# Four low parts of folded weights by TensorE and ScalarE, and layer 1's first statistics three products later

## The chip, the cores and the metric

The kernel runs on one core of one Trainium2 chip. The metric is the device time of one execution in microseconds (us). A core has five engines with instruction queues of their own: TensorE (PE; its weight loads are shown as PEld), VectorE (DVE), ScalarE (ACT), GpSimd (POOL) and SyncE (SP, which only issues transfers here). Each works through its queue in order and waits on semaphores for the others.

## The reference

A decoder trunk of two layers on x (1024 positions of width 1024), conditioned on a vector c. In short:

```python
c_act = silu(c)
for l in range(2):
    shift, scale, gate = split(c_act @ ada_w[l] + ada_b[l], 3)
    if l == 0:                                   # gated multi-scale causal pooling
        h = rmsnorm(x, norm_g[0]) * (1 + scale) + shift
        u, z = split(h @ w_in, 2)                # each 1024 x 2048
        p = trailing_mean(u, windows=(2, 4, 8, 16)) - u
        y = (einsum("sgc,gcd->sgd", p, w_group) * a_scale * silu(z)) @ w_out
    else:                                        # sliding-window attention, window 128, 16 heads
        k, v = from hk = modulated rmsnorm(x) @ w_kv   # shared K and V
        h = rmsnorm(x, norm_g[1]) * (1 + scale) + shift
        q, z = split(h @ b_w_in, 2)
        y = (attention(q, k, v, bias, sinks) * silu(z)) @ b_w_out
    x = x + gate * y
out = rmsnorm(x, final_g)
```

Pooling is linear along the positions, so for the first channel group the product of `w_in` and `w_group` can be formed ahead (`w_in @ w_group`, the "folded weights" below) and applied to h at once.

## The kernel before, in words

x is held transposed, as 8 tiles `xk[k]` of 128 channels by 1024 positions, and most work is done for two halves q of 512 positions. Every fp32 product is made of three passes of a faster format: a matrix is split in a high part (the value rounded to that format) and a low part (the rest), and high by high, high by low and low by high are summed in PSUM. "A product" below is one such pass, a 128x512 matmul.

The start. While x arrives, TensorE forms the folded weights for group 0: eight matrices `jb[m]` of 128x512 in PSUM banks (`join_mm`, line 629), each out of four chunks `ci` of `wu` and `wg`. Each is then split: `joined_h(m)` (line 634) copies it to SBUF as the high part by ScalarE, and `joined_l(m)` (line 639) subtracts that from the bank as the low part by VectorE. Meanwhile ScalarE squares x (715), VectorE sums the squares (720, 724), and for each half `rstd_stats` brings the sums over channels to PSUM (478, tiny matmuls against a column), VectorE adds the epsilon (`v`, 481), GpSimd raises it to the power -1/2 (`rs`, 483), and `rstd_spread` (490) spreads it over the partitions, from where ScalarE copies it (813 for the first half, 830 for the second). The shifts and scales of the adaptive norm are dot products of a loaded row block with silu(c) by VectorE (`ada_dot`, line 557; its bias comes from `pk`, a packed tile of small vectors; silu(c) is line 765, on the broadcast `cact`). Then for each k in 4, 0, ... the input of layer 0 is built for both halves: scaling (677, 680, VectorE), high part (682, ScalarE), low part (686, VectorE), and used at once in 12 products per k and half (`first_mm`, line 700) in the order (0,0), (0,1), (4,0), (4,1), (1,0) and so on.

Then follow layer 0's other products, its output projection in two parts (`ps_d` and others by line 985 and 530), and, before layer 1, the last chunks of the output projection for the second half of positions (`last_chunk`, 12 products each). Into their row on TensorE are put layer 1's first statistics (`rstd_stats` on `sqh[0]`) and their spread, whose result `rb` scales x for K, V and the queries.

What sets the order: up to the K and V products everything is noted first (`nc.noting`) and written out by a planner, `in_list`. TensorE's instructions keep the order of the source text. Those of ScalarE and VectorE are taken by a due time, `want`, counted back from the products that need them with estimated lengths; SP's transfers too. Instructions called through `at(t, f, ...)` near layer 1 are sorted by t ahead of that. Buffers are taken from rings by name, so an order also decides who waits for a buffer. From K and V on, a second list with its own planner follows; the change does not touch it.

Of the kernel before, what the change touches and what calls it, by code (L numbers as in the profile page):

```python
# [15 lines left out]
F32 = mybir.dt.float32  # L16
# [5 lines left out]
P = 128  # L22
# [80 lines left out]
LAG = {PE: 0.25, ACT: 0.15, DVE: 0.12, POOL: 0.12, SP: 0.0}  # L103


class Tile:


    def __init__(self, home, steps, on):
        self.home, self.steps, self.on = home, steps, on  # L110
# [100 lines left out]
class Step:  # L211
    def __init__(self, at, engine, length, kb, f, due):
        self.at, self.engine, self.length, self.kb, self.f = at, engine, length, kb, f
        self.due, self.lag = due, LAG[engine]
        self.needs, self.next, self.held, self.done, self.ready = set(), [], False, None, 0.0


# [67 lines left out]
def in_list(notes, begin):  # L285

    t = begin
    for n in notes:
        for m in n.needs:
            m.next.append(n)  # L290
        if n.engine == PE:
            n.want = t
            t += n.length
    left = {n: len(n.next) for n in notes}
    last_first = [n for n in notes if not left[n]]
    for n in last_first:
        for m in n.needs:
            left[m] -= 1
            if not left[m]:
                last_first.append(m)  # L300
    assert len(last_first) == len(notes)
    for n in last_first:
        if n.engine != PE:
            n.want = min([t + n.due] + [m.want for m in n.next]) \
                - n.length - n.lag - (n.kb / 250 + 2.0 if n.kb else 0.0)
    queue = [n for n in notes if n.engine == PE][::-1]
    by_want = {e: sorted((n for n in notes if n.engine == e), key=lambda n: (n.want, n.at))
               for e in (ACT, DVE)}
    left = {n: len(n.needs) for n in notes}
    free = dict.fromkeys(LAG, 0.0)  # L310
    free[PE], landed = begin, 0.0
    waiting = {e: [n for n in notes if n.engine == e and not left[n]] for e in LAG}

    def sooner(n, now):

        late = max(0.0, free[PE] - queue[-1].want) if queue else 0.0
        some = [m for m in by_want[n.engine][:40] if m.done is None and m.want < n.want][:10]
        for m in some:
            ready = now
            for o in m.needs:  # L320
                if o.done is not None:
                    ready = max(ready, o.done + o.lag)
                elif o.engine == PE:
                    ready = max(ready, max(o.want + late, free[PE]) + o.length + o.lag)
                else:
                    break
            else:
                end = now + n.length
                if now < ready < end - 0.05 and m.want + late < end < n.want + late - m.length:
                    return ready  # L330
        return None

    for _ in notes:
        while True:
            best = None
            for e, some in waiting.items():
                if e == PE:
                    some = queue[-1:] if queue and not left[queue[-1]] else []
                if some:
                    at = max(free[e], min(n.ready for n in some), landed - 2.5 if e == SP else 0.0)  # L340
                    n = min((n for n in some if n.ready <= at), key=lambda n: (n.want, n.at))
                    if best is None or at < best[0]:
                        best = at, n
            at, n = best
            then = None if n.held or n.engine not in by_want else sooner(n, at)
            if then is None:
                break
            n.held, free[n.engine] = True, then
        n.begin = at
        (queue.pop() if n.engine == PE else waiting[n.engine].remove(n))  # L350
        if n.engine in by_want:
            by_want[n.engine].remove(n)
        free[n.engine] = n.done = at + n.length
        if n.kb:
            landed = max(landed, n.done)
            landed += n.kb / (390 if 7.0 < landed < 45.0 else 300)
            n.done = landed + 2.0
        for m in n.next:
            left[m] -= 1
            m.ready = max(m.ready, n.done + (n.lag if m.engine != n.engine else 0.0))  # L360
            if not left[m] and m.engine != PE:
                waiting[m.engine].append(m)
    return sorted(notes, key=lambda n: (n.begin, n.at))
# [3 lines left out]
def trunk(ctx, tc, xT, x_again, c, pack, ada_first, ada_rest, wu0_in, wg0_in, wa, wg, wao, wkv,  # L367
          wb, wbo, bias_in, fg_row, outT, out_last):
    nc = Work(tc.nc)
    mm = nc.tensor.matmul  # L370
# [14 lines left out]
    def bank(tag):  # L385
        return pp.tile([P, H], F32, tag=tag, name="ps_" + tag, bufs=BANKS[tag])
# [23 lines left out]
    ident = cp.tile([P, P], F32, name="ident")  # L410
# [75 lines left out]
    def rstd_spread(rs, n):  # L486

        bc = bank("tp")
        for j in range(n):
            mm(bc[:, j * P:(j + 1) * P], rs[:, j:j + 1].broadcast_to([P, P]), ident,  # L490
               start=True, stop=True)
        return bc

    sqh = [None, None]
# [39 lines left out]
    with ExitStack() as sa:  # L534
# [10 lines left out]
        def slot(name):  # L545
            if not slots_at:
                slots_at.append(ap.tile([P, SLOT_FILL], F32, name="fill2"))
            return ap.tile([P, 2, H], F32R, tag="wo", name=name, bufs=4)
# [87 lines left out]
        def joined_l(*ms):  # L636
            for m in ms:
                w = w0[m // 2][:, m % 2]
                nc.vector.tensor_sub(out=w[:, 1, :], in0=jb[m], in1=w[:, 0, :].bitcast(F32))

        def dots(k, i, gain=True):
            ada_dot(ads[k][i], cact, 8 * i + k, C_ADAB + 8 * i + k)
# [48 lines left out]
        def first_mm(k, q, passes=(0, 1, 2)):  # L691
            if k == 0 and 0 in passes:
                for i in range(4):
                    psu[i, q] = bank(("d", ("tp", "o", "S", "S")[i])[q])
            order = [(s, i) for s in passes for i in range(4)]
            if (k, q) == (KT - 1, 1):
                order.sort(key=lambda e: e[1])
            for s, i in order:
                w, hl = ((0, 0), (1, 0), (0, 1))[s]
                mm(psu[i, q], w0[k // 2][:, k % 2, w, i * P:(i + 1) * P],  # L700
                   moving(block(k, q)[hl]),
                   start=k == 0 and s == 0, stop=k == KT - 1 and s == 2)
# [29 lines left out]
        nc.scalar.dma_start(raw0[:, half(0)], wu0_in[0, :, half(0)])  # L732
        fetch_c(0)
        nc.sync.dma_start(pk, pack)
        nc.sync.dma_start(cact, c.broadcast_to([P, T]))
        fetch_c(1)
        fetch_ada(0)
# [8 lines left out]
        def warm(n):  # L746

            some = ones.broadcast_to([P, P])
            for _ in range(n):
                mm(warm_bank[:, :P], some, some, start=True, stop=True)  # L750
# [3 lines left out]
                join_mm(m, jb[m], ci, s)  # L754

        warm(10)
        jb = [bank(t) for t in ("d", "d", "d", "d", "S", "S")]
        split_wg(0)
        split_wu(0, half(0), nc.vector.tensor_copy)
# [65 lines left out]
        first_l(0, 0)  # L825
        dots(4, 0, False)
        joined_h(7)
        joined_l(7)
        bc = rstd_spread(rs, 4)
        nc.scalar.copy(out=rbs[1], in_=bc)  # L830
        first_mm(0, 0)
        first_h(0, 1)
        dots(4, 1, False)
# [269 lines left out]
        w = split_w(*first_raw)  # L1103
# [6 lines left out]
        w = load_w(wa[17])  # L1110
# [109 lines left out]
        def g_acts(k, hl, q):  # L1220
            return moving(g_parts[8 + k, q][:, hl, :])
# [19 lines left out]
        for i, (kind, g, j) in enumerate(steps):  # L1241
            w, nxt = nxt, pair_w(*steps[i + 1]) if i + 1 < len(steps) else None
# [61 lines left out]

        late = list(range(LATE, KT))[::-1]

        def last_chunk(i):

            n, c = late[i // 2], i % 2
            if c == 0:  # L1310
                got[n] = bank(("S", "d")[i // 2 % 2])
            passes([(1, got[n])], ws[n], c * 512,
                   lambda k, hl, q: g_acts(4 * c + k, hl, q), 4, c == 0, c == 1)


        xrs = {}
# [34 lines left out]
        rb = slot("rb")[:, 0, :].bitcast(F32)  # L1351
        hk0 = Modulated(0, rb, 8, 48)
        h10 = Modulated(0, rb, 16, 24)
        got = {}
        plan = []

        def at(t, f, *args, due=12.0):
            plan.append((t, len(plan), f, args, due))

        def put(k, f, *args):  # L1360
            got[k] = f(*args)
# [22 lines left out]
        NT = 12 * 0.2157  # L1384
# [6 lines left out]
            at(t + 0.05, take_h, key, due=-0.2)  # L1391
            at(t + 1.3, take_l, key, due=0.2)
        for i in range(nl):
            at(NT * i, last_chunk, i)
            if i % 2 == 1:
                t, n = NT * (i + 1), late[i // 2]
                at(t + AFTER[0], lambda n: residual(n, 1, got[n], 16), n, due=3.0)
                at(t + AFTER[1], square_s, n, 1, due=3.0)
                at(t + AFTER[2], square_a, n, 1, due=3.0)
        assert rest_at[0] == len(rest_cols)  # L1400
        at(NT - 0.01, lambda: put("st", rstd_stats, sqh[0], 4))
        at(2 * NT - 0.01, lambda: nc.scalar.copy(out=rb, in_=rstd_spread(got["st"], 4)))
        for i in range(16):
            m = (hk0, h10)[i // 8]
            t = 2 * NT + STEP[0] + STEP[1] * i
# [989 lines left out]
```

## Time and profile before

| | us |
|---|---|
| median of 3 runs | 901.51 (901.36 to 901.70) |
| the profiled execution: time | 901.06 |
| the profiled execution: span, first to last instruction | 899.4 |
| TensorE busy | 889.5 (99%) |
| VectorE busy | 755.8 (84%) |
| ScalarE busy | 506.5 (56%) |
| GpSimd busy | 160.5 (18%) |
| mean granted TensorE clock | 0.998 |

Busy time of TensorE counts a product from its start to the end of its pipeline, so rows that follow one another overlap; a short wait hides in that. Lines are given as L and the number in the kernel before; the changed kernel has other numbers for the same statements (by 1 at the start, by 5 to 9 later).

### The profile page before, as it was taken

To read this page: it belongs to the slowest core of one execution; us is meant where nothing else is said; L and a number is where in the kernel's file an instruction comes from. 1 tells how busy PE (TensorE), PEld (TensorE's weight loads), DVE (VectorE), ACT (ScalarE), POOL (GpSimd) and SP (SyncE) were. 2 spreads that over 40 slices of the span, in tenths; PEclk is the share of its full clock that TensorE was granted. 3 is DMA by queue.
4 is the path that set the end of the run, shared out by engine and by line. 5 is a ranking of instruction groups with operands and counts; after the bars stand their busy time and mean duration, and the time that the engine had idled before them with its cause. 6 is when DMAs were issued, how large, how long until landed. Compare 5 with 4: busy or idle time off the path is not lost.

```text
span 899.4 us, 13251 instructions
## 1 busy us (share of the span) xinstructions
PE 889.5 (99%) x4486; PEld 787.3 (88%) x4486; DVE 755.8 (84%) x1411; ACT 506.5 (56%) x1074; POOL 160.5 (18%) x263
## 2 busy tenths in 40 slices
PE   9999999999999999999999999999999999999996
PEld 8788888888888888888888888888998888998996
DVE  6999989877988899698986789489999966779785
ACT  7546435333444335483353459488897656677643
POOL 0100000000000000000000000234434545456651
PEclk9999999999999999999999999999999999999999
DMA  9742451573248624998697966945777565465032
GB/s 360 275 140 94 166 209 48 190 244 127 94 171 310 255 84 141 320 345 305 223 325 272 338 239 231 321 152 204 237 258 274 186 204 166 159 194 184 16 141 105
DMA packets 65843, 186.80 MB, mean 208 GB/s; under 512 B 8168, under 2 KB 16496, under 8 KB 65776
## 3 DMA queue, kind: packets, MB, share of 16 engines
q1 hardware_dynamic: 56208, 151.88, 48.0%
q0 software_dynamic: 8992, 32.51, 10.9%
q10 hardware_dynamic: 576, 1.57, 0.5%
q8 instruction: 35, 0.57, 0.2%
q14 instruction: 32, 0.26, 0.1%
HBM read 138.48 MB, written 41.95 MB: 201 GB/s over the span
## 4 chain that ended last, share of the span: by engine, by line
PE 92%; DMA 4%; DVE 2%; issue 0%; ACT 0%; SPq 0%; DVEq 0%; ACTq 0%
PE ps_d L985 18%; PE ps_d L1581 9%; PE ps_d L1583 9%; PE ps_d L1582 9%; PE ps_S L985 9%; PE ps_d L530 9%; PE ps_tp L985 4%; PE ps_o L985 4%; PE ps_S L530 3%; PE ps_tp L530 2%; PE ps_o L530 2%; PE ps_d L700 2%; PE ps_o L1823 2%; PE ps_S L1736 2%; PE ps_tp L1773 2%; PE ps_S L1735 2%
## 5 line engine op out<-in xcount | busy, mean ns | idle before, releaser
L955 ACT CAST ws<-tw 128x512 fp32r<-128x512 f32 x68 | 41.5, 619 | 65.0 <-DVE tw L960 33.3
L985 PE MATMUL ps_d<-hs,ws 128*128 128x512 f32 x312 | 71.6, 379 | 0.0
L557 DVE CUSTOM_DVE_ANT_0 tmp<-tmp,cact,pk 128x1024 f32<-128x1024 f32 x48 | 60.6, 1278 | 9.0 <-DMA tmp<-ada_rest 9.0
L1581 PE MATMUL ps_d<-hm,wh 128*128 128x512 f32 x176 | 67.8, 385 | 0.0
L1582 PE MATMUL ps_d<-hm,wh 128*128 128x512 f32 x176 | 66.7, 379 | 0.0
L1583 PE MATMUL ps_d<-hm,wl 128*128 128x512 f32 x176 | 66.7, 379 | 0.0
L985 PEld LDWEIGHTS ps_d<-hs,ws 128*128 128x128 f32 x312 | 59.0, 189 | 8.4
L1750 ACT ACTIVATE P<-P,nm 128x129 f32<-128x129 f32 x128 | 50.1, 394 | 26.9 <-DVE nm L1746 26.6
L985 PE MATMUL ps_d<-ha,ws 128*128 128x512 f32 x252 | 57.8, 379 | 0.0
L872 POOL MEMSET tmp<- 128x16 f32 x12 | 1.3, 111 | 312.3 <-DMA kept_g<-tmp 137.1
L1791 POOL TENSOR_SCALAR_AFFINE_SELECT pp<-ph 128x512 fp32r<-128x512 f32 x54 | 46.1, 870 | 58.6 <-DVE ph L1779 38.4
L985 PEld LDWEIGHTS ps_d<-ha,ws 128*128 128x128 f32 x252 | 47.6, 189 | 6.8
L956 DVE TENSOR_TENSOR ws<-tw,ws 128x512 fp32r<-128x512 f32 x68 | 45.7, 683 | 7.3 <-ACT ws L955 7.2
L1791 POOL TENSOR_SCALAR_AFFINE_SELECT ph<-ph 128x512 fp32r<-128x512 f32 x56 | 45.5, 827 | 0.0
L956 DVE TENSOR_TENSOR ws<-raw,ws 128x512 fp32r<-128x512 f32 x51 | 34.7, 683 | 10.1 <-ACT ws L955 10.0
L1761 ACT ACTIVATE P<-P,den 128x128 f32<-128x128 f32 x128 | 40.6, 389 | 2.0 <-DVE den L1757 2.0
L483 POOL TENSOR_TENSOR rs<-v,mhalf 128x4 f32<-128x4 f32 x3 | 5.0, 1656 | 203.4 <-DVE v L481 203.4
L530 PE MATMUL ps_d<-gh,wh 128*128 128x512 f32 x128 | 40.9, 380 | 0.0
L955 ACT CAST ws<-raw 128x512 fp32r<-128x512 f32 x51 | 31.4, 620 | 12.1 <-issue 5.5
L1746 DVE CUSTOM_DVE_ANT_0 P<-ps_S,bias,nsink 128x128 f32<-128x128 f32 x128 | 37.7, 345 | 0.4
L1583 PEld LDWEIGHTS ps_d<-hm,wl 128*128 128x128 f32 x176 | 33.3, 189 | 4.7
L1581 PE MATMUL ps_d<-hm,raw 128*128 128x512 f32 x96 | 37.2, 387 | 0.0
(372 smaller groups left out, 2688.7 us busy)
## 6 DMA issues: line engine op xcount, KB each, us to landing
tmp<-ada_rest SPq DMA_DIRECT2D x48, 512.0 KB, 4.6
raw<-wa SPq DMA_DIRECT2D x28, 512.0 KB, 3.5
raw<-wao SPq DMA_DIRECT2D x21, 512.0 KB, 5.2
raw<-kw POOLq DMA_DIRECT2D x20, 512.0 KB, 4.3
wh<-kw POOLq DMA_DIRECT2D x19, 512.0 KB, 3.6
wl<-kw POOLq DMA_DIRECT2D x19, 512.0 KB, 4.6
ad<-ada_first SPq DMA_DIRECT2D x16, 512.0 KB, 4.4
kept_g<-tmp SPq DMA_DIRECT2D x16, 512.0 KB, 4.1
```

The lines of the kernel that those rows point to most:

```text
L530: mm(p, lhs, acts(k, hl, q), start=start and k == ks[0] and s == 0, stop=stop and k == ks[-1] and s == 2)
L557: nc.vector.tensor_tensor_reduce(out=raw, in0=raw, in1=ca, scale=1.0, scalar=pk[:, bcol:bcol + 1], op0=ALU.mult, op1=ALU.add, accum_out=ad ...
L955: nc.scalar.copy(out=ws[i][:, 0, :], in_=src)
L956: nc.vector.tensor_sub(out=ws[i][:, 1, :], in0=src, in1=ws[i][:, 0, :].bitcast(F32))
L985: mm(ps, lhs, acts(k, hl), start=start and k == 0 and s == 0, stop=k == 3 and s == 2, skip_group_check=True)
L1581: mm(p, lh, a[0](), start=k == 0, stop=False)
L1582: mm(p, lh, a[1](), start=False, stop=False)
L1583: mm(p, ll, a[0](), start=False, stop=k == n - 1)
L1746: note(DVE, 0.28, lambda: nc.vector.tensor_tensor_reduce(out=pt()[:, i, :P], in0=s()[:, e, :P], in1=bias[:, hd, :], scale=-1.0, scalar=nsi ...
L1750: note(ACT, 0.41, lambda: nc.scalar.activation(pt()[:, i, :P + 1], pt()[:, i, :P + 1], AF.Exp, bias=nm()[:, i:i + 1], scale=-1.0, accum_ou ...
L1761: note(ACT, 0.3, lambda: nc.scalar.activation(pt()[:, i, :P], pt()[:, i, :P], AF.Copy, scale=den()[:, i:i + 1]), [(den, i)], [(pt, i)])
L1791: note(POOL, 0.85, lambda: nc.gpsimd.affine_select(out=v8(to(), h), in_=v8(cur(), h).bitcast(F32), pattern=[[0, 2], [0, 4], [-sign, 2], [- ...
```

## The change

Four of the eight low parts, m = 2, 3, 6 and 7, are made by another way: TensorE multiplies the high part with a negated identity matrix (`less`) and adds this onto the bank, which leaves the low part there, and ScalarE copies it to SBUF. The last low part (m = 7) comes behind the second half's spread in the source. The transfer of `pk` gets a due time (`by`), which the planner keeps for it, and is issued ahead of the second half of x. Near layer 1, `last_chunk` is noted in four pieces of three products each instead of one of twelve, and the statistics and their spread are put one such piece, three products, later.

```diff
@@ Step, in_list
-        self.due, self.lag = due, LAG[engine]
+        self.due, self.lag, self.by = due, LAG[engine], float("inf")
...
+            n.want = min(n.want, n.by)
@@ trunk
         def joined_l(*ms):
             for m in ms:
                 w = w0[m // 2][:, m % 2]
-                nc.vector.tensor_sub(out=w[:, 1, :], in0=jb[m], in1=w[:, 0, :].bitcast(F32))
+                if m in (2, 3, 6, 7):
+                    mm(jb[m], less, w[:, 0, :], start=False, stop=True, skip_group_check=True)
+                    nc.scalar.copy(out=w[:, 1, :], in_=jb[m])
+                else:
+                    nc.vector.tensor_sub(out=w[:, 1, :], in0=jb[m], in1=w[:, 0, :].bitcast(F32))
...
         nc.sync.dma_start(pk, pack)
+        nc.notes[-1].by = 14.0
...
         warm(10)
+        less = slot("less")[:, 0, :P]
+        nc.scalar.mul(less, ident, -1.0)
...
         joined_h(7)
-        joined_l(7)
         bc = rstd_spread(rs, 4)
         nc.scalar.copy(out=rbs[1], in_=bc)
+        joined_l(7)
         first_mm(0, 0)
...
-        def last_chunk(i):
+        def last_chunk(i, ks=range(4)):
...
-            at(NT * i, last_chunk, i)
+            for k in range(4):
+                at(NT * (i + k / 4), last_chunk, i, range(k, k + 1))
...
-        at(NT - 0.01, lambda: put("st", rstd_stats, sqh[0], 4))
-        at(2 * NT - 0.01, lambda: nc.scalar.copy(out=rb, in_=rstd_spread(got["st"], 4)))
+        at(1.24 * NT, lambda: put("st", rstd_stats, sqh[0], 4))
+        at(2.24 * NT, lambda: nc.scalar.copy(out=rb, in_=rstd_spread(got["st"], 4)))
```

How instructions move. TensorE at the start, from the first half's statistics (`invd,first`) to the first product of layer 0 (`ha,w_131`); the rows by `wgs,wu` are the folded weights. Before:

```order
L478 MATMUL ps_o<-invd,first 128x1 x4
L629 MATMUL ps_S<-wgs,wu 128x512 x12
L490 MATMUL ps_tp<-ident,rs 128x128 x4
L629 MATMUL ps_S<-wgs,wu 128x512 x3
L478 MATMUL ps_o<-invd,second 128x1 x8
L629 MATMUL ps_S<-wgs,wu 128x512 x9
L490 MATMUL ps_tp<-ident,rs 128x128 x4
L700 MATMUL ps_d<-ha,w_131 128x512 x12
```

After, on the same stretch of TensorE:

```order
L479 MATMUL ps_o<-invd,first 128x1 x4
L641 MATMUL ps_d<-w_132,less 128x512 x2
L630 MATMUL ps_S<-wgs,wu 128x512 x12
L491 MATMUL ps_tp<-ident,rs 128x128 x4
L630 MATMUL ps_S<-wgs,wu 128x512 x3
L641 MATMUL ps_S<-w_134,less 128x512
L479 MATMUL ps_o<-invd,second 128x1 x8
L630 MATMUL ps_S<-wgs,wu 128x512 x9
L491 MATMUL ps_tp<-ident,rs 128x128 x4
L641 MATMUL ps_S<-w_134,less 128x512
L705 MATMUL ps_d<-ha,w_131 128x512 x12
```

Four products are added: two behind the first statistics, one ahead of the second, one behind the second spread.

VectorE at the start, from the first variance `v` on (`ISA ad,adac` is a dot, its next row reads the result; `w` are low parts, `second` sums of squares, `x<-x,acol` a scaling). Before:

```order
L481 TENSOR_SCALAR v<-ps_o 128x4
L720 TENSOR_TENSOR second<-second,tmp 128x1024
L639 TENSOR_TENSOR w_131<-ps_d,w_131 128x512
L720 TENSOR_TENSOR second<-second,tmp 128x1024
L639 TENSOR_TENSOR w_131<-ps_d,w_131 128x512
L639 TENSOR_TENSOR w_132<-ps_d,w_132 128x512
L557 ISA ad,adac<-ad,cact,pk 128x1024
L557 ISA adac 128x1
L481 TENSOR_SCALAR v<-ps_o 128x4
L557 ISA ad,adac<-ad,cact,pk 128x1024
L557 ISA adac 128x1
L677 SCALAR_TENSOR_TENSOR x<-x,acol,second 128x512
```

After, from the first variance on:

```order
L482 TENSOR_SCALAR v<-ps_o 128x4
L729 TENSOR_TENSOR second<-second,tmp 128x512
L725 TENSOR_TENSOR second<-second,tmp 128x1024 x2
L558 ISA ad,adac<-ad,cact,pk 128x1024
L558 ISA adac 128x1
L644 TENSOR_TENSOR w_131<-ps_d,w_131 128x512 x2
L682 SCALAR_TENSOR_TENSOR x<-x,acol,second 128x512
L482 TENSOR_SCALAR v<-ps_o 128x4
L558 ISA ad,adac<-ad,cact,pk 128x1024
L558 ISA adac 128x1
L558 ISA ad,adac<-ad,cact,pk 128x1024
L558 ISA adac 128x1
```

The low parts of `w_132` and `w_134` are gone from VectorE, those of `w_131` come behind the first dot, and the second variance comes behind the scaling and right ahead of two dots.

ScalarE at the start, from the squares of the second half on (`CAST w` at 634 or 635 is a high part, at 642 a copy of a low part). Before:

```order
L715 ACTIVATE second<-x 128x512 x2
L715 ACTIVATE tmp<-x 128x512 x5
L634 CAST w_131<-ps_d 128x512
L715 ACTIVATE tmp<-x 128x512
L634 CAST w_131<-ps_d 128x512
L765 ACTIVATE cact<-cact 128x1024
L634 CAST w_132<-ps_d 128x512
L813 COPY second<-ps_tp 128x512
L634 CAST w_132<-ps_d 128x512
L634 CAST w_134<-ps_S 128x512
L648 ACTIVATE acol<-adac,pk 128x1
L682 ACTIVATE ha<-x,adac 128x512
```

After, from the same squares on:

```order
L720 ACTIVATE second<-x 128x512 x2
L720 ACTIVATE tmp<-x 128x512
L635 CAST w_132<-ps_d 128x512 x2
L720 ACTIVATE tmp<-x 128x512 x5
L773 ACTIVATE cact<-cact 128x1024
L635 CAST w_134<-ps_S 128x512
L635 CAST w_131<-ps_d 128x512
L821 COPY second<-ps_tp 128x512
L635 CAST w_131<-ps_d 128x512
L653 ACTIVATE acol<-adac,pk 128x1
L642 CAST w_132<-ps_d 128x512 x2
L642 CAST w_134<-ps_S 128x512
```

The casts of `w_132` come up between the squares, that of `w_134` right behind silu(c), and three copies of low parts stand ahead of the first high part of layer 0's input (`ha`).

On SP's queue `pk` stood behind the sixteen loads of x, `cact` and two row blocks; now it stands behind the first eight loads of x. The small copies from `pk` into `asch` and `nsink` come up on VectorE from after layer 0's first products to ahead of the first variance. On TensorE near layer 1 the four `invd,sqh` matmuls and the four of the spread each stand behind three more products, with twelve products between the two as before.

More of the change, by code (lines that the diff above doesn't have):

```diff
@@ L1305, in trunk @@
         late = list(range(LATE, KT))[::-1]
-        def last_chunk(i):
+        def last_chunk(i, ks=range(4)):
             n, c = late[i // 2], i % 2
-            if c == 0:
+            if c == 0 and ks[0] == 0:
                 got[n] = bank(("S", "d")[i // 2 % 2])
             passes([(1, got[n])], ws[n], c * 512,
-                   lambda k, hl, q: g_acts(4 * c + k, hl, q), 4, c == 0, c == 1)
+                   lambda k, hl, q: g_acts(4 * c + k, hl, q), list(ks),
+                   c == 0 and ks[0] == 0, c == 1 and ks[-1] == 3)
         xrs = {}
```

## The prediction

> **What bounds the kernel now.** I read the chain that ended last first. In its rows (start, length, what) TensorE carries it from 43 us on, product after product; ahead of that stand a transfer and then VectorE.
>
> ```profile
> 18.65 7.90 DMA pk<-pack
> 26.69 1.28 DVE ad L557
> ...
> 43.86 2.59 PE ps_d L700 x12
> ```
>
> Twelve 128x512 products take 2.59 us, 0.216 us each. Then the busy time by stretch (length, then PE, PEld, DVE, ACT, POOL busy, clock, DMA share, GB/s):
>
> ```profile
> 30.00:40.00 10.00, 8.99 (x42) 6.93 (x43) 9.81 (x16) 4.65 (x8) 0.15 (x1) 1.00 0.54 202
> ...
> 515.00:520.00 5.00, 5.00 (x25) 4.38 (x24) 3.51 (x6) 0.64 (x1) 0.00 (x0) 1.00 0.98 375
> ```
>
> From 30 to 43 us VectorE is full and TensorE is not. The granted clock is 1.00 in these rows, so it is no term. TensorE's rows there (start, length, line; in brackets idle time and who ended it):
>
> ```profile
> 26.04 1.84 PE L478 MATMUL ps_o<-invd,second 128*128 128x1 f32 x16
> 27.74 2.19 PE L629 MATMUL ps_S<-wgs,wu 128*128 128x512 f32 x9
> 30.20 1.16 PE L490 MATMUL ps_tp<-ident,rs 128*128 128x128 f32 x8 [0.27 <-POOL rs L483]
> 31.11 2.84 PE L700 MATMUL ps_d<-ha,w 128*128 128x512 f32 x12
> 34.16 0.48 PE L700 MATMUL ps_tp<-a,w 128*128 128x512 f32 x1 [0.21 <-ACT a L682]
> 34.48 0.38 PE L700 MATMUL ps_o<-a,w 128*128 128x512 f32 x1
> ...
> 35.56 0.59 PE L700 MATMUL ps_S<-a,w 128*128 128x512 f32 x2
> 36.47 0.48 PE L700 MATMUL ps_tp<-a,w 128*128 128x512 f32 x1 [0.31 <-DVE a L686]
> ...
> 37.01 0.59 PE L700 MATMUL ps_S<-a,w 128*128 128x512 f32 x2
> 37.89 2.91 PE L700 MATMUL ps_d<-ha,w 128*128 128x512 f32 x12 [0.29 <-ACT ha L682]
> ...
> 41.93 0.59 PE L700 MATMUL ps_S<-ha,w 128*128 128x512 f32 x2
> 42.73 0.48 PE L700 MATMUL ps_tp<-ha,w 128*128 128x512 f32 x1 [0.21 <-DVE ha L686]
> 43.70 0.59 PE L700 MATMUL ps_d<-ha,w 128*128 128x512 f32 x2
> ```
>
> The brackets understate the loss, because a product's row is longer than its step. I count steps: a row's start plus its products at 0.216 is where the next could start. A product that follows a wait also delays its follower (34.16 to 34.48 is 0.32, not 0.22), 0.10 more; the first one after other kinds of work costs 0.08 more. The losses: before the spread 30.20 - (27.74 + 1.94 + 0.08) = 0.44; before 34.16, 0.38 + 0.10; before 36.47, 0.48 + 0.10; before 37.89, 0.45 + 0.10; before 42.73, 0.37 + 0.10. Together 2.52 us: all that a better start can win. From 43.70 on the chain runs along TensorE up to layer 1's statistics.
>
> **The four low parts and the order at the start.** VectorE's rows, whose starts give the true step of each kind:
>
> ```profile
> 24.11 1.21 DVE L720 TENSOR_TENSOR second<-second,tmp 128x1024 f32<-128x1024 f32 x1
> 25.24 1.28 DVE L639 TENSOR_TENSOR w<-ps_d,w 128x512 fp32r<-128x512 f32 x2
> ...
> 28.00 1.28 DVE L557 CUSTOM_DVE_ANT_0 ad<-ad,cact,pk 128x1024 f32<-128x1024 f32 x1
> ...
> 29.20 0.75 DVE L677 SCALAR_TENSOR_TENSOR x<-x,acol,second 128x512 f32<-128x512 f32 x1
> 29.86 0.68 DVE L639 TENSOR_TENSOR w<-ps_d,w 128x512 fp32r<-128x512 f32 x1
> ...
> 41.93 0.74 DVE L686 SCALAR_TENSOR_TENSOR ha<-x,adac,ha 128x512 fp32r<-128x512 f32 x1
> ```
>
> A dot is a step of 1.20 (28.00 to 29.20), a scaling (L677) 0.66, a sum of squares over 1024 columns (L720) 1.13; two low parts are 1.28 with the last one's tail, so one is a step of 0.60 (1.28 - 0.68). Four low parts leave VectorE: 2.4 us. TensorE gets 4 products of a kind it does not yet run (a negated identity against a high part). The nearest row is the ordinary product, 0.216: 0.86 in all; by the rows they cannot cost less than nothing nor more than 0.38 each. ScalarE gets 4 copies out of PSUM:
>
> ```profile
> 22.76 0.56 ACT L634 CAST w<-ps_d 128x512 fp32r<-128x512 f32 x1
> 23.23 0.63 ACT L715 ACTIVATE tmp<-x 128x512 f32<-128x512 f32 x1
> ...
> 24.22 1.06 ACT L765 ACTIVATE cact<-cact 128x1024 f32<-128x1024 f32 x1
> ```
>
> A copy is a step of 0.47 (22.76 to 23.23). The new negated identity is one 128x128 operation while ScalarE still waits for its first weights, at nothing; if that cover were gone it would cost below one copy, 0.47. The three small copies from pk that come up to VectorE (asch, nsink) fall where it waits for ScalarE's squares: nothing. On SP's queue pk passes eight loads of x; what was behind its old place moves up by as much as x was put back.
>
> Now the walk through the new order. TensorE: two extra products behind the first statistics and one ahead of the second: the second statistics begin at 26.04 + 3 x 0.216 = 26.69 and end at 28.39. ScalarE: the last square, at 23.23 behind one cast, now has two ahead of it: 23.23 + 0.47 = 23.70, done 24.33. VectorE: the last sum of squares waits for that square, and behind the sum ahead of it, which the two casts push as well: from 24.4 or a little later, 1.13 long. I take its end at 25.7, and the first dot starts there, not at 26.69, because pk no longer arrives at 26.55 but ahead of the second half of x. That half lands some 0.16 later for pk's 64 KB; ScalarE is busy, so this costs nothing up to about 0.2. Then dot, two low parts, a scaling: 25.7 + 1.20 + 1.20 + 0.66 = 28.76; only then the variance v, though TensorE had its sums at 28.5. GpSimd's power follows, and its length is the next question:
>
> ```profile
> 22.26 1.03 POOL L483 TENSOR_TENSOR rs<-v,mhalf 128x4 f32<-128x4 f32 x1 [19.88 <-DVE v L481]
> 28.16 1.99 POOL L483 TENSOR_TENSOR rs<-v,mhalf 128x4 f32<-128x4 f32 x1 [4.88 <-DVE v L481]
> ...
> 522.39 1.96 POOL L483 TENSOR_TENSOR rs<-v,mhalf 128x4 f32<-128x4 f32 x1 [178.63 <-DVE v L481]
> ...
> 570.82 1.04 POOL L2126 TENSOR_TENSOR rs<-v,mhalf 128x4 f32<-128x4 f32 x1 [2.54 <-DVE v L2124]
> ```
>
> It takes 1.0 or 2.0. In the second row VectorE had begun a dot at 28.00, and the power ends 0.87 after that dot (29.28); in the third VectorE had begun a subtraction at 522.25 (its row stands below), and the power ends 0.87 after it. In the new order a dot follows v at once again, so I take 1.99: from 28.98 to 30.97.
>
> The Trainium skill's page "SBUF — State Buffer", section "Who interferes with whom", says that a VectorE instruction with two SBUF inputs and a GpSimd instruction that reads SBUF contend, and that the one that issues first makes the other wait. The two long rows agree; that GpSimd ever held VectorE no row quoted here shows. By this rule the power waits for the dot and the sum is the one below; without it the power would take 1.03 and the sum would be 0.5 better.
>
> The spread starts at 31.03. TensorE is free at 28.39 + 0.08 + 9 x 0.216 = 30.41, so this wait grows from 0.44 to about 0.6. The spread takes 0.91 as before, the fourth extra product 0.22 (it waits for a cast that stands on ScalarE behind the first high part and is done at 31.4; all of layer 0's products queue behind it, wanted at 31.94), and the first layer-0 product starts at 32.2, 1.05 later than now. What follows is 48 products (the four blocks up to 43.70). Their inputs: the first high part waits for the second dot (30.1) and is ready at 30.9; the scaling of the second half waits for the spread's copy (32.8, VectorE idles 0.8 there), its high part comes at 34.3 where TensorE wants it at 34.8; the next ones are 0.6 early. The last, the low part of the row at 41.93, is in VectorE's chain 0.99 earlier by the early dot and 0.60 by low parts (three out, two in), and 0.65 later by more idling: it ends at 41.73 instead of 42.67. TensorE wants it at 41.65. So 0.1 to 0.2 may be left of that wait. The 48 products end at 32.2 + 10.36 = 42.55, or 42.7 with it, against 43.70.
>
> Term 1: -2.52 + 0.6 (wait before the spread) + 0.86 (extra products) = -1.06. The walk gives -1.0 to -1.15. I take -1.05. Its cover is thin on two sides: VectorE's chain and the spread.
>
> **Layer 1's statistics three products later.**
>
> ```profile
> 520.25 0.69 DVE L509 TENSOR_TENSOR sqh<-sqh,sq 128x512 f32<-128x512 f32 x1
> ...
> 520.55 0.38 PE L530 MATMUL ps_S<-gh,wl 128*128 128x512 f32 x1
> ...
> 521.08 1.02 PE L478 MATMUL ps_o<-invd,sqh 128*128 128x1 f32 x8 [0.15 <-DVE sqh L509]
> ...
> 522.25 1.23 DVE L1217 TENSOR_TENSOR tmp<-tmp,stage 128x1024 fp32r<-128x1024 f32 x1
> ...
> 524.64 1.05 PE L490 MATMUL ps_tp<-ident,rs 128*128 128x128 f32 x8
> ```
>
> The last product starts at 520.55, so the statistics could start at 520.77; they wait for the sum of squares until 521.08: 0.31 lost. Three products (0.65) put there cover it. The spread moves by three products too, so 12 products stay between them. Its input comes at 522.39 + 1.96 = 524.35, 0.29 ahead of 524.64, and both shift alike: still no wait. The modulated tiles get later by 0.3 to 0.65 against the products that read them; the tightest pair there has 2.5 us:
>
> ```profile
> 547.66 1.22 DVE L1378 TENSOR_TENSOR wl<-raw,wh 128x1024 fp32r<-128x1024 f32 x1
> ...
> 551.43 0.38 PE L517 MATMUL ps_d<-hm,wh 128*128 128x512 f32 x1
> ```
>
> Term 2: -0.31. The ends: -0.31, and nearly +0.4 against the shifted TensorE if what the sum waits for does not come earlier with it (rival c).
>
> **Sum.** -1.05 - 0.31 = -1.36 on the profiled 901.06 us: 899.7. That run lies 0.45 below the median of 901.51, and the median is what will be compared: 901.51 - 1.36 = 900.15. What can be told from no change here is about 0.2%, 1.8 us; all gaps gone with the extra products paid would be -2.52 + 0.86 - 0.31 = -1.97, just over it.
>
> **Rivals.** (a) The power runs in 1.03: the spread's wait falls to nothing, 0.5 more: 899.6. For it speak the two short rows, against it the dot right behind v. (b) The power waits out two dots, since the new order has two in a row where now a scaling follows the first: 1.2 more before the spread and before VectorE's second scaling, and term 1 falls to about +0.1: 901.3. Against it: the scaling that began at 29.20, ahead of the first dot's end, did not keep the power from ending at 30.15. (The rule of the Trainium skill's page "SBUF — State Buffer" named above does not say who comes next when both wait; taken against GpSimd it gives this case.) (c) Term 2 is lost to the transfers: their share is 0.98 at 515 to 520 us. If the landings stay where they are while TensorE comes 1 us earlier, the sum of squares stays at 520.95 and the wait moves there; only the three products' 0.65 are won in all: 900.9. Against it: the transfers are issued behind VectorE's and ScalarE's work, which comes earlier too. (d) The other side. The extra product ahead of the second statistics waits for a cast that stands behind the activation of c, and that for c's broadcast:
>
> ```profile
> 16.68 0.33 SPq L735 DMA_DIRECT2D cact<-c  x1
> ...
> DMA to landing us min/median/max: 7.2/7.2/7.2
> ```
>
> It lands at 23.9, 24.1 with pk ahead of it; cast and product end the chain 1.6 later, at 25.7, and TensorE wants it at 26.5. So it is free up to 0.7 us; beyond that every microsecond of lateness stops TensorE in its order, and the gain is gone at 2.1 us late and 1.8 us lost at 3.9: 903.3. Nothing in the row speaks for so late a landing.
>
> **How the numbers follow.** The forecast, with term 1 from -0.7 to -1.3, 0.64 (900.15, own range 899.7 to 900.8); (a) 0.13; (b) 0.07; (c) 0.08; (d) and other mishaps 0.05; 0.03 for a gain below all gaps that I can name. Faster by over 0.2% means under 899.7: most of (a), the 0.03 and the edge of the forecast, 0.2. Slower over 0.2%: 0.05 with (d). The rest, 0.75, is the same. The range for 8 in 10 goes from 899.3, beyond (a), to 901.5, beyond (b).
>
> **What would show it.** In the trace after: the first dot at 25.7 and not at pk's landing; the power at 29.0 for 2.0; the spread at 31.0 with a wait of about 0.6 us before it; from 32.2 TensorE without gaps, at 42.6 where it is now at 43.70; layer 1's eight statistics rows without a wait in front. I am wrong if the power's length or start differs by half a microsecond, if the extra products are not 0.216 each, or if a gap stays between 32 and 43 us.

## The result, and the profile after

The changed kernel takes 900.03 us (median of 18 runs, 899.48 to 900.77) against 901.43 us of the kernel before in the same runs (18, 901.04 to 902.44): 1.40 us less, ratio 0.9983 with a 95% interval of 0.9977 to 0.999. The forecast was 900.15. The two profiled executions differ by less: 900.07 against 901.06, 0.99 us. The working below goes by them.

TensorE's rows of the kernel after at the start, to be read against the rows from 26.04 to 43.70 in the prediction (start, length, line, tiles, count, in brackets idle time and who ended it):

```profile
26.58 0.40 PE L641 MATMUL ps_S<-w,less 128*128 128x512 f32 x1
26.82 1.84 PE L479 MATMUL ps_o<-invd,second 128*128 128x1 f32 x16
28.52 2.19 PE L630 MATMUL ps_S<-wgs,wu 128*128 128x512 f32 x9
31.39 1.16 PE L491 MATMUL ps_tp<-ident,rs 128*128 128x128 f32 x8 [0.68 <-POOL rs L484]
32.30 0.48 PE L641 MATMUL ps_S<-w,less 128*128 128x512 f32 x1
32.62 2.75 PE L705 MATMUL ps_d<-ha,w 128*128 128x512 f32 x12
...
42.14 0.48 PE L705 MATMUL ps_tp<-ha,w 128*128 128x512 f32 x1
42.46 0.38 PE L705 MATMUL ps_o<-ha,w 128*128 128x512 f32 x1
...
43.10 2.75 PE L705 MATMUL ps_d<-ha,w 128*128 128x512 f32 x12
```

From 32.62 to 43.10 the brackets of before are gone: 48 products in 10.48 us, where they took 12.59 (31.11 to 43.70). The wait before the spread has grown. VectorE's and GpSimd's rows say why:

```profile
26.05 1.28 DVE L558 CUSTOM_DVE_ANT_0 ad<-ad,cact,pk 128x1024 f32<-128x1024 f32 x1
...
27.26 1.29 DVE L644 TENSOR_TENSOR w<-ps_d,w 128x512 fp32r<-128x512 f32 x2
28.46 0.74 DVE L682 SCALAR_TENSOR_TENSOR x<-x,acol,second 128x512 f32<-128x512 f32 x1
29.12 0.15 DVE L482 TENSOR_SCALAR v<-ps_o 128x4 f32<-128x4 f32 x1
29.19 1.27 DVE L558 CUSTOM_DVE_ANT_0 ad<-ad,cact,pk 128x1024 f32<-128x1024 f32 x1
...
30.39 1.28 DVE L558 CUSTOM_DVE_ANT_0 ad<-ad,cact,pk 128x1024 f32<-128x1024 f32 x1
```

```profile
29.35 1.99 POOL L484 TENSOR_TENSOR rs<-v,mhalf 128x4 f32<-128x4 f32 x1 [5.99 <-DVE v L482]
```

TensorE's second statistics ended at 28.52, but v stands on VectorE behind a dot, two low parts and a scaling, and is made at 29.12. The power then ends (31.34) 0.88 after the dot that follows v (30.46).

Layer 1, first VectorE's sum of squares, then TensorE around the statistics:

```profile
519.66 0.69 DVE L510 TENSOR_TENSOR sqh<-sqh,sq 128x512 f32<-128x512 f32 x1
```

```profile
520.61 0.38 PE L531 MATMUL ps_S<-gh,wl 128*128 128x512 f32 x1
520.82 0.95 PE L479 MATMUL ps_o<-invd,sqh 128*128 128x1 f32 x8
521.63 0.68 PE L531 MATMUL ps_S<-gh,wh 128*128 128x512 f32 x2
```

The step into the statistics is 0.21 instead of 0.53, and the statistics themselves take 0.81 (to 521.63) where they took 0.89 (521.08 to 521.97): 0.40 less.

### The profile page after: what moved, and what is told of

Same layout as the page of the kernel before. It is cut to its first block, busy times and chain, and to the rows that moved or that the text cites. A ratio compares the mean times of both kernels' runs of the same rounds, so it can differ in the third digit from the quotient of the medians.

```text
span 898.4 us, 13258 instructions
## 1 busy us (share of the span) xinstructions
PE 889.3 (99%) x4490; PEld 787.9 (88%) x4490; DVE 754.1 (84%) x1407; ACT 508.6 (57%) x1079; POOL 160.7 (18%) x263
## 4 chain that ended last, share of the span: by engine, by line
PE 97%; DVE 1%; ACT 0%; issue 0%; POOL 0%; DVEq 0%; ACTq 0%
PE ps_d L993 18%; PE ps_d L1591 9%; PE ps_d L1593 9%; PE ps_d L1592 9%; PE ps_d L531 9%; PE ps_S L993 9%; PE ps_o L993 4%; PE ps_tp L993 4%; PE ps_S L531 3%; PE ps_tp L531 3%; PE ps_o L531 3%; PE ps_d L705 2%; PE ps_o L1833 2%; PE ps_S L1746 2%; PE ps_tp L1783 2%; PE ps_S L1745 2%
```

## The experiments

Times are medians; "before" is the kernel before, run beside each. The block is the first layer-0 product that stood at 43.70 before and at 43.10 after, in each profiled execution; statistics are the second half's on TensorE. In the code of the experiments, `nc.notes[-1]` is the instruction noted last, and `needs` holds the instructions that the planner must place ahead of one.

| kernel | us | before | ratio, 95% interval | statistics | spread | block |
|---|---|---|---|---|---|---|
| lows_only | 900.57 | 901.75 | 0.9987 (0.9978 to 0.9996) | 26.70 | 31.01 | 42.73 |
| pk_only | 901.42 | 901.75 | 0.9997 (0.9988 to 1.0006) | 26.04 | 30.20 | 43.71 |
| move_only | 901.01 | 901.75 | 0.9993 (0.9985 to 1.0002) | 26.39 | 31.06 | 44.57 |
| v_first | 899.84 | 901.75 | 0.9982 (0.9973 to 0.9991) | 26.88 | 30.61 | 42.62 |
| no_pk | 899.83 | 901.41 | 0.9983 (0.9974 to 0.9992) | 26.35 | 30.94 | 42.66 |
| after_again | 900.31 | 901.41 | 0.9985 (0.9977 to 0.9994) | 26.73 | 31.20 | 42.92 |
| low7_late | 899.71 | 901.41 | 0.9980 (0.9972 to 0.9989) | 26.79 | 30.52 | 42.43 |
| v_scale | 899.48 | 901.41 | 0.9980 (0.9971 to 0.9989) | 26.49 | 30.22 | 42.23 |
| mid7 | 899.61 | 901.51 | 0.9979 (0.9970 to 0.9988) | 26.88 | 30.61 | 42.47 |
| v_scale_again | 899.84 | 901.51 | 0.9982 (0.9973 to 0.9991) | 26.60 | 30.33 | 42.34 |

An interval is 1.6 us wide, so the times separate few of these from one another; the verdicts rest on the rows. The statistics column shows how far the first loads shift a single execution: 26.60 and 26.49 in one kernel, 26.82 and 26.73 in another.

**lows_only.** The low parts alone: the diff of the change without `nc.notes[-1].by = 14.0` and without the `last_chunk` part.

> The four low parts by TensorE and ScalarE alone; pk is fetched where it was, layer 1 is as before. Theory A (the low parts carry the start's gain and the early pk gives none): the first dot waits for pk until 26.7, so VectorE has only one low part between it and the second v; v comes at about 28.6 instead of 29.12, the spread at about 30.9 instead of 31.39, and the block that starts at 43.70 before and at 43.10 after starts at 42.6 to 42.7: 1.0 less than before. Theory B (the prediction's walk: the low parts give 0.60 and the early dot 0.99 on VectorE's chain): without the early dot that block comes later than with the whole change, at 43.2 or after. Layer 1's wait before its statistics stays at 0.3 in both.

VectorE, then TensorE:

```profile
26.93 1.28 DVE L558 CUSTOM_DVE_ANT_0 ad<-ad,cact,pk 128x1024 f32<-128x1024 f32 x1
...
28.74 0.15 DVE L482 TENSOR_SCALAR v<-ps_o 128x4 f32<-128x4 f32 x1
```

```profile
31.01 0.71 PE L491 MATMUL ps_tp<-ident,rs 128*128 128x128 f32 x4 [0.41 <-POOL rs L484]
...
42.73 0.81 PE L705 MATMUL ps_d<-ha,w 128*128 128x512 f32 x3
```

The dot is 0.88 later than after the whole change, yet v comes at 28.74 instead of 29.12, the spread at 31.01 and the block at 42.73, 0.97 ahead of before. Theory A holds: the low parts carry the start's gain. Theory B, by which an early dot is worth 0.99, falls.

**pk_only.** Only `nc.notes[-1].by = 14.0` with its two lines in the planner.

> pk is fetched after the first eight loads of x, and nothing else changes. Theory A: the dot moves ahead of one low part and starts near 25.9 instead of 26.69, but the second v waits for TensorE's statistics (until 27.74) and stays at 27.9, the power waits for the dot that follows it and the spread stays at 30.2; the block at 43.70 moves by less than 0.15, and the time by less than 0.2. Theory B: VectorE's chain is 0.8 to 1.0 ahead from the first dot on, the waits before 36.47, 37.89 and 42.73 shrink, and the block starts near 42.9.

VectorE, then TensorE:

```profile
25.98 1.28 DVE L558 CUSTOM_DVE_ANT_0 ad<-ad,cact,pk 128x1024 f32<-128x1024 f32 x1
...
27.18 0.69 DVE L640 TENSOR_TENSOR w<-ps_d,w 128x512 fp32r<-128x512 f32 x1
27.92 0.16 DVE L482 TENSOR_SCALAR v<-ps_o 128x4 f32<-128x4 f32 x1
```

```profile
30.20 1.16 PE L491 MATMUL ps_tp<-ident,rs 128*128 128x128 f32 x8 [0.27 <-POOL rs L484]
...
43.71 0.59 PE L701 MATMUL ps_d<-ha,w 128*128 128x512 f32 x2
```

The dot starts 0.71 earlier, a low part takes the place behind it, and v waits for TensorE as before. The spread and the block stand where they stood, within 0.01. Theory A again. (The median is 0.33 lower than before's, and its interval includes no change.)

**move_only.** Only the part on `last_chunk` and the two lines `1.24 * NT` and `2.24 * NT`.

> Layer 1's statistics and spread three products later, nothing else. By the trace after, where the step to the statistics is 0.21 instead of 0.53 and the statistics' own run is 0.81 instead of 0.89: 0.40 less than before from layer 1 on, nothing at the start, so 901.1 where the kernel before is 901.5. By the rival (the wait is given back in the next stage, because the residual products end three products earlier or the loads saturate): no gain by 530.

Its profiled execution is the slowest of its 11 (901.86). VectorE, then TensorE at the start and at layer 1:

```profile
27.58 1.28 DVE L558 CUSTOM_DVE_ANT_0 ad<-ad,cact,pk 128x1024 f32<-128x1024 f32 x1 [0.31 <-DMA pk<-pack]
```

```profile
26.39 1.84 PE L479 MATMUL ps_o<-invd,second 128*128 128x1 f32 x16
...
31.06 0.60 PE L491 MATMUL ps_tp<-ident,rs 128*128 128x128 f32 x3 [0.78 <-POOL rs L484]
...
522.07 0.38 PE L531 MATMUL ps_S<-gh,wl 128*128 128x512 f32 x1
522.29 0.95 PE L479 MATMUL ps_o<-invd,sqh 128*128 128x1 f32 x8
523.10 0.68 PE L531 MATMUL ps_S<-gh,wh 128*128 128x512 f32 x2
```

Layer 1 is as expected: a step of 0.22 into the statistics and 0.81 through them, and nothing of it is given back by 530. The start, which this kernel leaves alone, shows something else. On SP's queue:

```profile
19.59 0.33 SPq L735 DMA_DIRECT2D pk<-pack  x1
```

pk was issued 0.94 later than in the profile of before (18.65), because the sixteen loads of x ahead of it on SP's queue took 12.40 to issue instead of 11.46. It then took as long to land (7.8 and 7.9), so it landed 0.9 later (27.4 against 26.55), the dot waited for it, and the spread came 0.86 later although TensorE's statistics were only 0.35 later. So in the old order the start does depend on pk when pk is late, and gains nothing, by pk_only's rows, when pk is earlier than it was. In before the two chains end together: the dot at 27.90, and v, which waits for TensorE, starts at 27.92.

**v_first.** The whole change, and on VectorE one low part behind the second v instead of ahead of it. The diff is against the changed kernel:

```diff
-        joined_l(1)
+        joined_l(1); low_1 = nc.notes[-1]
...
-        at_v = nc.notes[-2]
+        at_v = nc.notes[-2]; low_1.needs.add(at_v)
...
-        nc.notes[-1].needs.add(at_v)
+        nc.notes[-1].needs |= {at_v, low_1}
```

> The whole change, and one low part (m = 1) moved on VectorE from ahead of the second v to behind it and ahead of the dot that now follows v. The low part reads PSUM and SBUF, the dot two tiles of SBUF. If the power is held by an instruction that reads two SBUF tiles: v at 28.6 instead of 29.12, the power takes 1.03 instead of 1.99 and ends at 29.95, the spread starts when TensorE is free (30.46) instead of 31.39, and the block at 43.10 starts at 42.3 to 42.4, 0.7 less than after. If the power takes 2.0 whatever stands beside it: it ends at 30.9, the spread starts at 30.95, and the block starts at 42.65, 0.45 less than after.

VectorE, GpSimd, TensorE:

```profile
28.76 0.16 DVE L482 TENSOR_SCALAR v<-ps_o 128x4 f32<-128x4 f32 x1
28.84 0.68 DVE L644 TENSOR_TENSOR w<-ps_d,w 128x512 fp32r<-128x512 f32 x1
29.44 1.27 DVE L558 CUSTOM_DVE_ANT_0 ad<-ad,cact,pk 128x1024 f32<-128x1024 f32 x1
```

```profile
29.00 1.01 POOL L484 TENSOR_TENSOR rs<-v,mhalf 128x4 f32<-128x4 f32 x1 [5.59 <-DVE v L482]
```

```profile
30.61 1.05 PE L491 MATMUL ps_tp<-ident,rs 128*128 128x128 f32 x8
31.45 0.49 PE L641 MATMUL ps_S<-w,less 128*128 128x512 f32 x1
32.07 2.86 PE L705 MATMUL ps_d<-ha,w 128*128 128x512 f32 x12
```

The power takes 1.01 beside a low part, and the spread no longer waits. The block comes 0.48 earlier than after the whole change, not 0.7: a new wait of 0.40 stands before the first layer-0 product (32.07; free at 31.67). Its high part comes from a dot that is 0.25 later now, and stands on ScalarE behind the cast for m = 7.

**no_pk and after_again.** no_pk is the changed kernel without the line `nc.notes[-1].by = 14.0`; after_again is the changed kernel itself.

> The whole change without the early fetch of pk (the low parts and layer 1's later statistics remain). Theory A (with the low parts gone, an early dot draws a low part and a scaling ahead of the second v and so delays the spread): start as in the low parts alone, v at 28.7, spread at 31.0 where the whole change has 31.39, the block after the first 48 layer-0 products at 42.7 where it has 43.10, and layer 1's 0.40 on top: 0.4 faster than the whole change when pk lands at 26.8. Rival (the early pk is worth its place because in many executions pk lands late, at 27.4 in one profile, and the dot then waits): the median is no better than that of the whole change run beside it, though a profile with pk at 26.8 is.

> The changed kernel once more, as the yardstick of the three others on the same chip: 1.0 faster than before by the two profiles, 1.4 by the medians so far. Its profile repeats v at 29.1, the power at 1.99, the spread at 31.4 and the block at 43.1, each within the 0.4 by which the start of the loads varies.

The start without the early pk has v at 28.68 and the block at 42.66, after_again at 28.93 and 42.92: 0.26 between them where 0.4 was expected, and TensorE's statistics were 0.38 earlier in no_pk, which is more than the whole of it. Counted from the statistics to the block, no_pk takes 16.31, the changed kernel 16.28 and 16.19, and lows_only, the other kernel with the late pk, 16.03. On VectorE v follows TensorE's sums by 0.63 in no_pk (28.05 to 28.68), where it stands behind the late dot, by 0.60 and 0.50 in the changed kernel, where it stands behind the scaling, and by 0.33 in lows_only. So the two kernels without the early pk do not agree on whether it costs anything in the new order, and theory A is not shown here. The medians differ by 0.48 in favour of no_pk, with intervals that overlap. The rival, that the early pk is worth its place by the median, finds no support either. What the early pk is worth in the new order stays open.

**v_scale, v_scale_again.** The whole change, with the first scaling behind v and ahead of the dot; both low parts stay ahead. The diff is against the changed kernel:

```diff
-        nc.notes[-1].needs.add(at_v)
+        nc.notes[-1].needs.add(at_v); dot_00 = nc.notes[-1]
...
-        first_h(0, 0)
+        first_h(0, 0); nc.notes[-2].needs.add(at_v); dot_00.needs.add(nc.notes[-2])
```

> The whole change, with the first scaling of the first layer-0 block moved on VectorE from ahead of the second v to behind it, ahead of the dot; both low parts stay ahead. The scaling, like the dot, reads two tiles of SBUF. If the power is held only by the one VectorE instruction that has started before it: it waits for the scaling (0.67) and takes about 1.35, the spread starts when TensorE is free (30.5), and the block at 43.10 starts at 42.5 to 42.6. If it is held by every such instruction in a row: it waits for the scaling and the dot, takes 2.6, and the spread starts at 31.5, no better than now.

> The changed kernel with v ahead of the scaling once more, as the yardstick on the same chip: the power takes 1.45, the spread starts with TensorE free, and the median is 0.4 to 0.8 below the changed kernel's 900.0 to 900.3.

VectorE, GpSimd, TensorE of v_scale:

```profile
28.37 0.16 DVE L482 TENSOR_SCALAR v<-ps_o 128x4 f32<-128x4 f32 x1 [0.25 <-PE ps_o L479]
28.45 0.74 DVE L682 SCALAR_TENSOR_TENSOR x<-x,acol,second 128x512 f32<-128x512 f32 x1
29.11 1.28 DVE L558 CUSTOM_DVE_ANT_0 ad<-ad,cact,pk 128x1024 f32<-128x1024 f32 x1
```

```profile
28.61 1.45 POOL L484 TENSOR_TENSOR rs<-v,mhalf 128x4 f32<-128x4 f32 x1 [5.52 <-DVE v L482]
```

```profile
31.68 1.56 PE L705 MATMUL ps_d<-ha,w 128*128 128x512 f32 x6
```

The power ends at 30.06, 0.87 after the scaling's end (29.19), while the dot runs from 29.11 to 30.39. So the power waits for the one VectorE instruction that had started before it, not for a row of them. From the statistics to the block it takes 15.74 us in both runs (26.49 to 42.23, 26.60 to 42.34), the changed kernel 16.28 and 16.19: 0.45 to 0.54 for one scaling moved by one place. The wait that is left is the one for the first high part (31.68). This kernel was faster than the one before both times, by 1.93 and 1.67 us; beside the changed kernel it was 0.83 us ahead (899.48 against 900.31), with overlapping intervals, and the 0.4 to 0.8 expected of its second run became 0.2 to 0.5. That it is faster than the changed kernel rests on the rows, not on the times.

**low7_late.** v_first, and the fourth extra product behind the first twelve layer-0 products. The diff is against v_first:

```diff
-        joined_l(7)
         first_mm(0, 0)
+        joined_l(7)
```

> As with v ahead of the low part of m = 1, and the fourth extra product (m = 7) and its copy moved behind the first twelve layer-0 products, so that ScalarE makes the first high part ahead of the cast that this product waits for. In the run before, TensorE stood from 31.67 to 32.07 for that high part (31.29 to 32.01 on ScalarE, behind the cast). Theory: the high part starts at 30.75 and the first layer-0 product at 31.5; the extra product costs its 0.22 later; the block that stood at 42.54 starts at 42.0 to 42.1, so 0.4 to 0.5 less, unless VectorE's chain (0.3 of room at the low part of 41.5) takes back up to 0.2. Rival: VectorE's chain is the bound again and nothing is gained.

```profile
31.44 2.86 PE L705 MATMUL ps_d<-ha,w 128*128 128x512 f32 x12
34.13 0.40 PE L641 MATMUL ps_S<-w,less 128*128 128x512 f32 x1
...
34.79 0.89 PE L705 MATMUL ps_S<-a,w 128*128 128x512 f32 x2
35.52 0.38 PE L705 MATMUL ps_tp<-a,w 128*128 128x512 f32 x1
```

The first layer-0 product starts at 31.44 as expected, but the block comes only 0.19 earlier than in v_first (0.10 with its statistics' 0.09 taken off), where 0.4 to 0.5 was expected: the extra product takes 0.23 behind the block, and the second of the two products at 34.79 waits (0.73 to 35.52 for two) for the bank of m = 7, which ScalarE's copy now leaves later (34.56 to 35.15). The rival named VectorE's chain; it was the bank.

**mid7.** v_scale, with the first high part ahead of the cast for m = 7 on ScalarE, and the fourth extra product behind four layer-0 products, ahead of that bank's next use. The diff is against v_scale:

```diff
-        first_h(0, 0); nc.notes[-2].needs.add(at_v); dot_00.needs.add(nc.notes[-2])
+        first_h(0, 0); nc.notes[-2].needs.add(at_v); dot_00.needs.add(nc.notes[-2]); high_00 = nc.notes[-1]
...
-        joined_h(7)
+        joined_h(7); nc.notes[-1].needs.add(high_00)
...
-        joined_l(7)
-        first_mm(0, 0)
+        first_mm(0, 0, (0,)); joined_l(7)
+        first_mm(0, 0, (1, 2))
```

> As with v ahead of the scaling, and two things more: ScalarE makes the first high part ahead of the cast for m = 7, and the fourth extra product comes after the first four layer-0 products instead of ahead of them. In the run before it, TensorE stood 0.40 at 31.28 for that high part (30.91 to 31.63 on ScalarE), and had 0.08 of waiting left at 41.50, where VectorE's low part is the last to come. Theory: the first layer-0 product starts at about 31.2 instead of 31.68, but the low part at 41.2 is only 0.1 to 0.2 earlier, since VectorE's chain from the second v on is full again; 0.1 to 0.2 less than its yardstick, the rest of the 0.5 is waited for near 41. Rival: VectorE's chain keeps up, and the whole 0.4 to 0.5 is gained.

VectorE, then TensorE:

```profile
28.76 0.16 DVE L482 TENSOR_SCALAR v<-ps_o 128x4 f32<-128x4 f32 x1 [0.25 <-PE ps_o L479]
...
40.70 0.75 DVE L691 SCALAR_TENSOR_TENSOR ha<-x,adac,ha 128x512 fp32r<-128x512 f32 x1
```

```profile
41.00 0.59 PE L705 MATMUL ps_S<-ha,w 128*128 128x512 f32 x2
41.50 0.48 PE L705 MATMUL ps_tp<-ha,w 128*128 128x512 f32 x1
41.82 0.38 PE L705 MATMUL ps_o<-ha,w 128*128 128x512 f32 x1
```

From the statistics to the block it takes 15.59 us, v_scale_again 15.74: 0.15 less, as the theory had it, with a wait still there for VectorE's low part, which ends at 41.45 (41.00 to 41.82 is three products, 0.65, and 0.17 of wait). In the profiles the block is 0.13 later all the same, because the statistics were 0.28 later, and the medians (899.61 and 899.84) do not separate. In this kernel VectorE's rows from v at 28.76 to that low part follow one another without a wait: from the second v on, VectorE's chain bounds the start.

## Why the prediction held, and where it did not

The time is within 0.12 us of the forecast and the direction is right, but two of its steps were off, and the agreement is partly luck.

Term 1 was -1.05 and is -0.60 in the profiled executions. By its own parts:

| | forecast | measured |
|---|---|---|
| second statistics later, by three extra products | +0.65 | +0.78 (26.04 to 26.82) |
| growth of the wait before the spread | +0.16 | +0.41 (0.44 to 0.85) |
| fourth extra product, spread to first layer-0 product | +0.22 | +0.32 (0.91 to 1.23) |
| waits in the 48 products gone | -2.08 | -2.11 (12.59 to 10.48) |

The last row, the mechanism, was right, with 0.12 left of the waits (10.48 against 48 products at 0.216, 10.36), at 42.14, where 0.1 to 0.2 was expected. Of the first row's 0.78, 0.08 is not the extra products': the first half's statistics already began 0.08 later (21.02 and 21.10). The largest miss is the second row. The step that failed is the walk's "25.7 + 1.20 + 1.20 + 0.66 = 28.76" for v: the first dot began at 26.05 and not at 25.7, behind the last sum of squares, and the same three steps then gave 29.12 for v. The walk also took the early dot for a gain of 0.99 in VectorE's chain. pk_only and lows_only show that it is none: in the old order, with pk landing as in before's profile, v waits for TensorE whatever the dot does, and in the new one the early dot lets a scaling come ahead of v (in lows_only it comes behind v). v_scale, where v stands ahead of that scaling, has v 0.17 behind TensorE's sums (28.20 to 28.37); in the changed kernel it is 0.60 (28.52 to 29.12), so the scaling makes v 0.43 later there. The start's gain came with the low parts: lows_only has it without the early pk. The extra products were mis-sized as well: by their steps the product at 26.58 took 0.24 and that at 32.30 took 0.32, not 0.216. About 0.1 of the second is no new cost: in before it fell to the first layer-0 product, then the first behind the spread, whose row of twelve took 2.84 (31.11) and takes 2.75 now (32.62).

The power's length was right, 1.99, and for the reason given. Rival (a), a power of 1.03, did not come with the change. v_first has such a power (1.01), and its block gains 0.48 where the rival had 0.5; that they agree is partly chance, since v_first's v also came 0.36 earlier and 0.40 went into the new wait for the first high part. Rival (b) fell with the changed kernel itself: two dots follow v, the second from 30.39 to 31.67, and the power ended at 31.34, 0.88 after the first.

The Trainium skill's page "SBUF — State Buffer", section "Who interferes with whom", has a VectorE instruction with two SBUF inputs and a GpSimd instruction that reads SBUF contend. The traces agree for the power: 1.99 behind a dot, 1.45 behind a scaling, 1.01 beside a low part, which reads PSUM and SBUF. That VectorE is made to wait in turn, when the power was first, no run here shows: in v_first the dot began at 29.44, while the power ran until 30.01, and took its usual 1.27, and in before a sum of squares of two SBUF tiles began at 22.37, 0.11 after the first power (22.26 to 23.29), and took 1.22, as the next one did (24.11, 1.21).

Term 2 was -0.31 and is -0.40: the wait went as forecast, and the statistics' own row is 0.08 shorter when nothing waits in front of it, which the term left out. Rival (c) fell: the sum of squares came 0.59 earlier (520.25 to 519.66), as much as TensorE did. Rival (d) did not occur: the product at 26.58 follows its predecessor without a wait. It was nearer than the prediction had it, though: c's broadcast landed at about 24.6 instead of 24.1, and the cast that the product needs ended at 26.18, so 0.40 of the room of 0.7 was left.

So the sum is -1.00 in the profiles, against -1.36; the profiled execution took 900.07 where the prediction's own sum gives 899.7. The medians differ by 1.40 in the first 18 runs and by 1.10 when the changed kernel was run again. The profiled execution of before was 0.37 below its median, that of after 0.04 above, while the prediction let both medians lie equally far above their profiles. These 0.4 make up for what the sum lacks: that the median comes so near to the forecast is luck. Two things were seen to lengthen single executions: move_only's late pk at the start, and a wait for a transfer in layer 1's attention that neither profile above has, here in after_again:

```profile
692.19 0.38 PE L1843 MATMUL ps_o<-pp,vd 128*128 128x256 f32 x1 [0.16 <-DMA pp<-pp]
```

A row of 0.38 instead of 0.28 for such a product stands in move_only (693.70) and low7_late (683.13) too. What it costs can be worked out: the time of a profiled execution less the start of its block is 857.35 to 857.42 in the three kernels without the later statistics (before, lows_only, pk_only), 856.97 to 857.09 in six runs with them, and 857.29 to 857.39 in after_again, move_only and low7_late. So term 2 is 0.26 to 0.45 in nine executions, and one such wait costs 0.2 to 0.4. Whether the late pk and these waits make up the 0.4 between profiles and medians in the executions without a profile was not shown.

## What to carry to other kernels

Work taken off a full engine gains only where a wait ends on it: ask what the engine puts next into the room, since here the scheduler filled it with a scaling ahead of the one small instruction that a chain over three engines hung on. When several engines take turns (sums, variance, power, spread), move the small links ahead of everything that can wait, and then look at what stands just behind them: one place on VectorE was worth 0.5 us here, beside 0.6 us that the whole change brought at the start. And before crediting a transfer that lands earlier, check that its reader was the last to be waited for; alone it brought nothing in its profile.

## What the runs showed of the hardware that was not expected

- GpSimd's power of 128x4 (1.01 to 1.04 alone) ends 0.87 to 0.88 us after the end of the VectorE instruction with two SBUF inputs that had started before it, whatever starts next: 1.99 behind a dot, 1.45 behind a scaling.
- The eight statistics columns of layer 1 take 0.81 on TensorE when they follow a product directly and 0.89 after a wait.
- A VectorE instruction with two SBUF inputs that starts while the power runs is not lengthened: the dot at 29.44 in v_first (1.27) and the sum of squares at 22.37 in before (1.22).
- In two executions of one order (before and move_only), SP took 11.46 and 12.40 us to issue the sixteen loads of x, so that pk behind them was issued, and landed, 0.9 us later; why the issues differ is open.
